# Memory stage of an encoder trunk: sums of squares by one-column matmuls, and another order of requests and reads

## The chip, the core and the metric

The kernel runs on one core of a Trainium2 chip. Its engines are TensorE (PE; its weight loads are shown as PEld), VectorE (DVE), ScalarE (ACT), GpSimd (POOL) and SyncE (SP), which issues most transfers. The metric is device time of one execution in microseconds.

## What is computed

Two layers of an encoder on 1024 tokens of width 1024. The change lies in the part that comes first: the projection of 256 memory tokens for both layers, and the first RMSNorm of the tokens.

```python
mem_n = rmsnorm(mem, norm_mem)
for i in range(DEPTH):
    h = rmsnorm(x, norm_mix[i])
    mkv = mem_n @ w_mem_kv[i]
    mk = mkv[..., :mw].reshape(B, N_MEM, N_MEM_HEADS, HEAD_DIM)
    mv = mkv[..., mw:].reshape(B, N_MEM, N_MEM_HEADS, HEAD_DIM)
    ...
    proj = h @ w_in_a[li]
    ...

def rmsnorm(x, g):
    x32 = x.astype(jnp.float32)
    y = x32 * lax.rsqrt(jnp.mean(x32 * x32, axis=-1, keepdims=True) + EPS)
    return (y * g.astype(jnp.float32)).astype(x.dtype)
```

After it come windowed attention with the first projection's results, memory attention, the output projection, a gated channel mixer, then the same with neighbourhood attention, and a last norm.

## The kernel before

All activations lie transposed: a tile has 128 features in its partitions and tokens along its free dimension. Tokens `x[k][f]` are 8 feature tiles by 2 halves of 512 tokens; memory tokens `memt` are 8 tiles of 256 tokens. A matrix product is made nearly exact in float32 by splitting each operand in a high part (a rounded copy, ScalarE, `hi`, L106) and a low part (the difference, VectorE, `lo`, L109), and by three products for each pair of tiles (`three`, `steps`, the matmul at L139). A dense unit has 8 feature tiles, so 24 products.

The memory stage works in the pool `mp`:

- The requests for memory tokens, the first weight unit `wm0`, the gains and the second unit go out first; unit 0's two halves are on ScalarE's queue, everything else on SyncE's.
- ScalarE multiplies each memory tile with its gain and rounds it (L293), VectorE makes the low part (L294). The product is made with tokens that are not yet normalized; the scale of the norm is applied to the result.
- `mem_norm` adds up squares: ScalarE squares a tile (L196), VectorE adds it to the sum so far (`merge`, L219), so that one tile is left. `mean` (L212) multiplies 128-column blocks of it, as weights, with a column of 1/1024, which leaves the mean square of each token in a partition. `scale` then adds epsilon (VectorE, L232), raises to the power -1/2 (GpSimd, L233), spreads the result over a diagonal (VectorE, L235) and broadcasts it by a product with ones (L242).
- A loop of eight units follows, four for each layer (two of keys, two of values). In round `i` it requests and splits unit `i + 2`, requests two or three token tiles, multiplies unit `i` (`dense`), and reads the result at once, with the scale (L337). Keys are split; values are transposed first (L344). Rounds 1 and 2 square the first token half, `norms[0]`; rounds 5 and 6 the second, `norms[1]`. From round 3 on, two tiles of the first half are normalized (L259) and split in each round.
- `first_dense` multiplies the first three units of the first projection with the first half (72 products 512 wide), while the second half is normalized; `first_units` in layer 0 then multiplies the same weights with the second half (72 more). The first score product of the attention (L559) comes after it.

A planner lays instructions out for each engine ahead of time; it keeps dependences, and takes what it expects to be ready in the order of the program. Each engine runs its list in that order and stops at what is not ready. A tag with `bufs` buffers gives a tile the buffer of an earlier one once that is done with: weights in split form (`whl`) have 3, unsplit ones (`raw`) 5, temporary tiles (`t2k`) 8. PSUM has 2 banks for `mm`, 2 for `S`, 3 for `T` and 1 for `O`; `mm_tile` gives results of units banks of the first three by turns, and the means of a norm hold a `T` bank until they are read.

The class `Norm` already has a number `summed`: tiles beyond that many are not added up but go to `mean` one by one. Its default is 8, all tiles.

```python
            self.acc.append(sq)
            if len(self.xs) > 2:
                self.merge()
```

Of the kernel before, what the change touches and what calls it, by code (L numbers as in the profile page):

```python
# [9 lines left out]
F32 = mybir.dt.float32  # L10
F32R = mybir.dt.float32r
AF = mybir.ActivationFunctionType
ALU = mybir.AluOpType
# [4 lines left out]
P = 128  # L18
D = 1024
S = 1024  # L20
NK = D // P
HS = 512
HD = 64
NH = 12
NKV = 4
NMH = 4
NM = 256
# [14 lines left out]
def trunk_kernel(ctx: ExitStack, tc: tile.TileContext, a: dict, out: bass.AP):  # L42
# [17 lines left out]
    nc = tc.nc  # L60
# [4 lines left out]
    wp = pool("wp", bufs=1)  # L65
# [4 lines left out]
    ps_t = pool("ps_t", bufs=3, space=PSUM)  # L70
    ps_o = pool("ps_o", bufs=1, space=PSUM)
# [10 lines left out]
    ident = cst.tile([P, P], F32, name="ident")  # L82
    gains = cst.tile([P, 6, NK], F32, name="gains")
    sink = cst.tile([P, NH], F32, name="sink")
    nsink = cst.tile([P, NH], F32, name="nsink")
    ones = cst.tile([P, P], F32, name="ones")
# [14 lines left out]
    def raw_tile(name):  # L101

        return phase[0].tile([P, D], F32, tag="raw", name=name, bufs=phase[2])

    def hi(dst, src):
        nc.scalar.copy(dst, src)  # L106

    def lo(dst, src, h, eng=None):
        (eng or nc.vector).tensor_tensor(dst, src, h.bitcast(F32), op=ALU.subtract)  # L109

    def load_w(src, tag="whl", bufs=3, eng=None, name="w", pool=wp, parts=1):
        raw = raw_tile(f"{name}_raw")
        nc.sync.dma_start(raw, src)
        w = pool.tile([P, 2, D], F32R, tag=tag, name=name, bufs=bufs)
        for i in range(parts):
            c = slice(i * D // parts, (i + 1) * D // parts)
            hi(w[:, 0, c], raw[:, c])
            pieces = 4 if eng is nc.gpsimd else 1
            for j in range(pieces):
                n = D // parts // pieces  # L120
                cj = slice(i * D // parts + j * n, i * D // parts + (j + 1) * n)
                lo(w[:, 1, cj], raw[:, cj], w[:, 0, cj], eng)
        return w
# [25 lines left out]
    def run_some(g, n):  # L149
        for _ in range(n):  # L150
            next(g, None)

    def first_dense(layer, norm):

        pre = []
        src = a["w_in_a"] if layer == 0 else a["w_in_b"]
        todo = (norm.add(x[k][1]) for k in range(len(norm.xs), NK))
        parts = norm.split(layer, hT[1])
        for n, u in enumerate(FIRST[layer]):
            w = load_w(src[u], eng=None if layer == 0 else nc.gpsimd, name="wf")  # L160
            wide[:] = True, 2 + n
            ps = mm_tile()
            for i, _ in enumerate(steps(ps, w, hT[0])):
                if next(todo, 0) is not None and len(norm.xs) == NK and (n or i > 3):
                    next(parts, None)
            pre.append((w, ps))
        run(parts)
        return pre
# [10 lines left out]
    def dense(w, h, n=HS):  # L179
        ps = mm_tile()  # L180
        run(steps(ps, w, h, n=n))
        return ps
# [85 lines left out]
    x = [[None, None] for _ in range(NK)]  # L268


    with tc.tile_pool(name="mp", bufs=1, reuse_waits="tile") as mp:
        phase[:] = mp, 8, 5
        memt = mp.tile([P, NK, NM], F32, name="memt")
        warm = mp.tile([P, P], F32, name="warm")
        nc.scalar.activation(warm, ones, AF.Square)
        wm0 = raw_tile("wm0")
        nc.sync.dma_start(memt[:, :2], a["mem"][:, :2])
        nc.scalar.dma_start(wm0[:, :HS], a["w_mem"][0, 0][:, :HS])
        nc.sync.dma_start(gains, a["gains"])
        nc.sync.dma_start(memt[:, 2:4], a["mem"][:, 2:4])  # L280
        nc.scalar.dma_start(wm0[:, HS:], a["w_mem"][0, 0][:, HS:])
        nc.sync.dma_start(memt[:, 4:], a["mem"][:, 4:])
        w0 = wp.tile([P, 2, D], F32R, tag="whl", name="wm", bufs=3)
        hi(w0[:, 0, :HS], wm0[:, :HS])
        lo(w0[:, 1, :HS], wm0[:, :HS], w0[:, 0, :HS])
        ws = [w0]


        mh = []
        mhl = mp.tile([P, NK, 2, NM], F32R, name="mhl")  # L290
        for k in range(NK):
            t, g = mhl[:, k], gains[:, 4, k : k + 1]
            nc.scalar.activation(t[:, 0], memt[:, k], AF.Copy, scale=g)  # L293
            nc.vector.scalar_tensor_tensor(  # L294
                t[:, 1], memt[:, k], g, t[:, 0].bitcast(F32), op0=ALU.mult, op1=ALU.subtract
            )
            mh.append(t)
            if k == 1:
                hi(w0[:, 0, HS:], wm0[:, HS:])
                lo(w0[:, 1, HS:], wm0[:, HS:], w0[:, 0, HS:])  # L300
        ws.append(load_w(a["w_mem"][0, 1], name="wm"))
        nc.sync.dma_start(ident, a["ident"])

        def load_x(f, k):
            x[k][f] = mp.tile([P, HS], F32, tag=f"x{k}{f}", name=f"x0_{k}{f}")
            nc.sync.dma_start(x[k][f], a["x"][k][:, f * HS : (f + 1) * HS])

        mem_norm = Norm(NM)
        for k in range(NK):
            mem_norm.add(memt[:, k])  # L310
        scale = mp.tile([P, NM], F32, name="mscale")
        nc.scalar.copy(scale, mem_norm.scale())

        hT = [[None] * NK, [None] * NK]
        norms = [Norm(), Norm()]
        kept = []
        for i in range(8):
            l, u = divmod(i, 4)
            if u == 0:
                kh = mp.tile([P, 2, NM], F32R, name=f"mkh{l}", tag="mkh", bufs=2)  # L320
                kl = mp.tile([P, 2, NM], F32R, name=f"mkl{l}", tag="mkl", bufs=2)
                vm = mp.tile([P, 2, NMH, 2, HD], F32R, name=f"mv{l}", tag="mv", bufs=2)
                kept.append((kh, kl, vm))
            if i + 2 < 8:
                ws.append(load_w(a["w_mem"][(i + 2) // 4, (i + 2) % 4], name="wm"))
            if i == 0:
                nc.sync.dma_start(sink, a["sink"].to_broadcast([P, NH]))
                nc.vector.tensor_scalar(nsink, sink, -1.0, None, op0=ALU.mult)
            if i < 3:
                for k in ((0, 1, 2), (3, 4, 5), (6, 7))[i]:  # L330
                    load_x(0, k)
            elif i < 7:
                for k in (2 * i - 6, 2 * i - 5):
                    load_x(1, k)
            ps = dense(ws[i], mh, NM)
            t = temp("mt", NM)
            nc.vector.tensor_tensor(t, ps[:, :NM], scale, op=ALU.mult)  # L337
            if u < 2:
                hi(kh[:, u], t)
                lo(kl[:, u], t, kh[:, u])  # L340
            else:
                tr = ps_t.tile([P, HS], F32, tag="T", name="mvT")
                for b in range(2):
                    nc.tensor.transpose(tr[:, b * P : (b + 1) * P], t[:, b * P : (b + 1) * P], ident)  # L344
                src = tr[:, :NM].rearrange("p (b i d) -> p b i d", b=2, i=2)
                m = 2 * (u - 2)
                for b in range(2):
                    hi(vm[:, b, m : m + 2, 0], src[:, b])
                    lo(vm[:, b, m : m + 2, 1], src[:, b], vm[:, b, m : m + 2, 0])
            if i in (1, 2):  # L350
                for k in range(4 * i - 4, 4 * i):
                    norms[0].add(x[k][0])
            if i == 2:
                parts = norms[0].split(0, hT[0])
            if i > 2:
                run_some(parts, 2)
            if i in (5, 6):
                for k in range(4 * i - 20, 4 * i - 16):
                    norms[1].add(x[k][1])
        pre = first_dense(0, norms[1])  # L360
        for l, (kh, kl, vm) in enumerate(kept):
            nc.sync.dma_start(memk_d[l, 0], kh.rearrange("p m k -> p (m k)").bitcast(F32))
            nc.sync.dma_start(memk_d[l, 1], kl.rearrange("p m k -> p (m k)").bitcast(F32))
            nc.sync.dma_start(memv_d[l], vm.rearrange("p b m i d -> p (b m i d)").bitcast(F32))

    for layer in range(2):
# [427 lines left out]
        with (  # L794
# [24 lines left out]
            norms = [Norm(), Norm()]  # L819
# [216 lines left out]
            for f in range(2):  # L1036
                for m in range(NK):
# [3 lines left out]
                    if f == 0 and m in po:  # L1041
                        w, ps = wo[m], po[m]
                        run(steps(ps, w, yT[f], [last_pair], start=False))
                    else:
                        ps = mm_tile("po")
                        w = wo[m] if f == 0 and m in wo else load_w(a["w_out"][layer, m], name="wo")
# [6 lines left out]
                    if f == 1 and m == 0:  # L1053
                        parts = norms[0].raw(2 + layer)
                    if f == 1:
                        k = next(parts)
# [114 lines left out]
            kept, left, right = {}, {}, {}  # L1171
# [181 lines left out]
            norms = [Norm(), Norm() if is_a else Norm(HS, 7)]  # L1353
            dorder = [(i, g) for i in (0, 1, 3, 2, 4, 5, 6) for g in range(len(groups))]
            parts = iter(())
# [124 lines left out]
```

## Time and profile before

| | us |
|---|---|
| three runs | 2146.28, 2148.43, 2148.71 |
| their median | 2148.43 |
| the profiled execution | 2144.64 |
| span of its instructions | 2142.7 |
| TensorE busy in that span | 2100.1 |
| first product of the memory stage | at 5.74 |
| first score product of layer 0 | at 83.90 |

The page of the profile gives busy times, the span in 40 slices of 54 us, the chain that ended last, and groups of instructions. The timeline gives runs of like instructions: start, time, engine, line, operation, result and operands, shape, count, and in brackets the idle time before them with what ended it. A view by windows gives busy time of the engines in a stretch, the granted TensorE clock and the load of the transfer engines. "L106" is line 106 of the kernel before.

### The profile page before, as it was taken

What the parts mean: (1) busy time and instruction counts of PE and PEld (TensorE: products, weight loads), DVE (VectorE), ACT (ScalarE), POOL (GpSimd) and SP (SyncE); (2) the same over time, 40 slices, a digit from 0 to 9 for tenths busy, and PEclk for the clock granted to TensorE, in tenths of its full rate; (3) what the DMA queues carried; (4) which work ended last, traced back from release to release, by engine and by line L of the source; (5) the groups of instructions that cost most, each with busy time, mean ns of one, the idle gap of its engine ahead of it and who ended that gap; (6) DMA issues with size and microseconds to landing.
All of it is one profiled execution on the core that took longest, in us unless ns stands there. A gap on an engine that the chain in (4) does not pass through costs nothing.

```text
span 2142.7 us, 28954 instructions
## 1 busy us (share of the span) xinstructions
PE 2100.1 (98%) x10270; PEld 1749.9 (82%) x10270; DVE 1514.4 (71%) x2466; ACT 1062.1 (50%) x2034; POOL 577.2 (27%) x617
## 2 busy tenths in 40 slices
PE   7999999999999999999999999999999999999997
PEld 6788888788888888888778888887888888888886
DVE  7677787788666666867766666667886666677675
ACT  6577785444433434344466566653443434344442
POOL 0344330334443430000233233203243444410000
PEclk9999999999999999999999999999999999999998
DMA  6321018323322336865232222265133323267562
GB/s 249 101 94 49 32 60 295 118 84 123 106 92 103 109 113 244 303 215 197 96 97 65 73 62 71 88 251 162 56 118 112 108 96 111 99 251 262 200 206 93
DMA packets 120080, 287.27 MB, mean 134 GB/s; under 512 B 12288, under 2 KB 18688, under 8 KB 119936
## 3 DMA queue, kind: packets, MB, share of 16 engines
q1 hardware_dynamic: 112896, 272.57, 37.5%
q10 hardware_dynamic: 7040, 12.85, 1.6%
q8 instruction: 81, 1.33, 0.3%
q14 instruction: 63, 0.52, 0.1%
HBM read 210.40 MB, written 68.94 MB: 130 GB/s over the span
## 4 chain that ended last, share of the span: by engine, by line
PE 77%; issue 13%; DVE 4%; ACT 3%; POOL 2%; DMA 1%; SPq 0%; DVEq 0%; ACTq 0%; POOLq 0%
PE X L885 16%; PE Y L885 16%; PE mm L139 14%; PE po L139 8%; PE X L1308 6%; PE Y L1308 4%; PE S L559 3%; PE O L622 3%; PE pT L602 3%; PE X L967 2%; PE Y L967 2%; ACT p L574 1%; DVE pl L109 1%; POOL wS L842 1%; DMA wm_raw<-in_w_mem 1%
## 5 line engine op out<-in xcount | busy, mean ns | idle before, releaser
L885 PE MATMUL Y<-hB,wgu 128*128 128x512 f32 x1056 | 256.1, 392 | 0.8 <-ACT c L905 0.8
L885 PE MATMUL X<-hB,wgu 128*128 128x512 f32 x1056 | 254.6, 390 | 0.0
L1308 PE MATMUL X<-hB,wd 128*128 128x512 f32 x1056 | 242.4, 390 | 1.1 <-DVE x L1276 1.1
L109 DVE TENSOR_TENSOR wgu<-wS,wgu 128x1024 fp32r<-128x1024 f32 (+1 forms) x124 | 152.9, 1233 | 124.9 <-ACT wgu L106 124.8
L1308 PEld LDWEIGHTS X<-hB,wd 128*128 128x128 f32 x1056 | 197.9, 188 | 43.2 <-issue 2.4
L885 PEld LDWEIGHTS Y<-hB,wgu 128*128 128x128 f32 x1056 | 196.6, 188 | 43.2 <-ACT c L905 1.6
L885 PEld LDWEIGHTS X<-hB,wgu 128*128 128x128 f32 x1056 | 196.1, 188 | 40.0
L587 POOL TENSOR_SCALAR p<-p,stat 128x384 f32<-128x384 f32 (+1 forms) x256 | 140.9, 569 | 314.5 <-DVE stat L584 205.2
L139 PE MATMUL mm<-hT,wqk 128*128 128x512 f32 x672 | 199.9, 405 | 0.1
L106 ACT CAST wgu<-wS 128x1024 fp32r<-128x1024 f32 (+1 forms) x124 | 114.3, 923 | 148.6 <-POOL wS L842 124.5
L139 PE MATMUL po<-yT,wo 128*128 128x512 f32 x768 | 184.7, 394 | 0.0
L1308 PE MATMUL Y<-hB,wd 128*128 128x512 f32 x792 | 180.4, 389 | 0.0
L1308 PEld LDWEIGHTS Y<-hB,wd 128*128 128x128 f32 x792 | 148.6, 188 | 31.2 <-DVE x L1276 0.3
L233 POOL TENSOR_TENSOR nr<-nv,neg_half 128x4 f32<-128x4 f32 (+1 forms) x11 | 11.7, 1063 | 597.6 <-DVE nv L232 597.5
L139 PEld LDWEIGHTS po<-yT,wo 128*128 128x128 f32 x768 | 142.4, 188 | 29.6 <-issue 1.0
L885 PE MATMUL X<-hT,wgu 128*128 128x512 f32 x624 | 150.1, 391 | 0.0
L106 ACT CAST hB<-b_raw 128x512 fp32r<-128x512 f32 x154 | 89.5, 618 | 110.8 <-DMA b_raw<-b_d 97.4
L842 POOL TENSOR_TENSOR wS<-wgu_raw 128x512 f32<-128x512 f32 x44 | 61.0, 1386 | 294.5 <-DVE wgu L109 294.5
L574 ACT ACTIVATE p<-p,stat 128x256 f32<-128x256 f32 (+1 forms) x192 | 112.3, 586 | 52.6 <-DVE stat L570 49.9
L885 PEld LDWEIGHTS X<-hT,wgu 128*128 128x128 f32 x624 | 116.9, 188 | 26.1
L109 DVE TENSOR_TENSOR pl<-pT,ph 128x384 fp32r<-128x384 f32 (+1 forms) x256 | 118.7, 494 | 21.0 <-ACT ph L106 17.9
L109 DVE TENSOR_TENSOR hB<-b_raw,hB 128x512 fp32r<-128x512 f32 x154 | 100.0, 688 | 42.3 <-ACT hB L106 42.0
(179 smaller groups left out, 4229.6 us busy)
## 6 DMA issues: line engine op xcount, KB each, us to landing
wgu_raw<-in_w_gu SPq DMA_DIRECT2D x92, 512.0 KB
wd_raw<-in_w_dn SPq DMA_DIRECT2D x70, 512.0 KB
b_raw<-b_d SPq DMA_DIRECT2D x70, 512.0 KB
b_d<-c SPq DMA_DIRECT2D x88, 256.0 KB
b_d<-t SPq DMA_DIRECT2D x66, 256.0 KB
wo_raw<-in_w_out SPq DMA_DIRECT2D x32, 512.0 KB
x<-in_x SPq DMA_DIRECT2D x32, 256.0 KB
xr_d<-x ACTq DMA_DIRECT2D x32, 256.0 KB
```

What stands on the lines that cost most here:

```text
L106: nc.scalar.copy(dst, src)
L109: (eng or nc.vector).tensor_tensor(dst, src, h.bitcast(F32), op=ALU.subtract)
L139: nc.tensor.matmul(ps[:, :n], l, r, start=start and i == 0 and j == 0, stop=stop and i == len(order) - 1 and j == 2,)
L559: nc.tensor.matmul(s_[:, :n], Q[self.h][:, qb * P : (qb + 1) * P], k, start=j == 0, stop=j == 1)
L574: nc.scalar.activation(p[:, :n], p[:, :n], AF.Exp, bias=m1, scale=-1.0, accum_out=s1)
L587: nc.gpsimd.tensor_scalar(p[:, :n], p[:, :n], ri[:, i : i + 1], 1.0, op0=ALU.mult, op1=ALU.mult)
L602: nc.tensor.transpose(tr[:, j * P : (j + 1) * P], p[:, j * P : (j + 1) * P], ident)
L622: nc.tensor.matmul(o[:, c0 : c0 + w * P], self.value(j), t[:, s0 : s0 + w].rearrange("p j q -> p (j q)"), start=j == js[0] and t is self.p ...
L842: sub = lambda o, p_, q_: nc.gpsimd.tensor_tensor(o, p_, q_, op=ALU.subtract)
L885: nc.tensor.matmul(ps, l, r, start=n in (0, 1, 3, 6) and k == 0 and i == 0, stop=k == 3 and i == 2, skip_group_check=True,)
L967: nc.tensor.matmul(bank[:, at : at + h2], l, r, start=start and k == 0 and i == 0, stop=stop and k == 1 and i == 2, skip_group_check=True,)
L1308: nc.tensor.matmul(bank, l, r, start=i in (0, 1, 3, 6) and p == 0 and n == 0, stop=p == HF - 1 and n == 2, skip_group_check=True,)
```

## The change

- Five products of `ones` with `ones` stand at the head of TensorE's list.
- Token requests are made for two feature tiles at once (512 KB) and stand earlier: the four of the first half between those of weight units 1, 2 and 3, the four of the second half with units 4 to 7. Weight units are requested four rounds ahead (before: two), and still split two rounds ahead.
- The three norms of the stage are made with `summed` 0: every squared tile goes to `mean` itself, and no `merge` is left in them.
- Squaring of the first token half stands ahead of the products of rounds 1 and 2, before behind them. The scale of the memory norm stands behind the product of round 2, before ahead of the loop.
- Results are read in a function of their own, `finish_wm`: unit 0 in round 2, unit `i - 2` in each later round, units 6 and 7 after the loop.
- The request for the sink logits stands behind those of unit 3 and of the first token half.

```diff
@@ -273,21 +273,50 @@
         memt = mp.tile([P, NK, NM], F32, name="memt")
         warm = mp.tile([P, P], F32, name="warm")
         nc.scalar.activation(warm, ones, AF.Square)
-        wm0 = raw_tile("wm0")
+        for _ in range(5):
+            nc.tensor.matmul(ps_o.tile([P, HS], F32, tag="O", name="warm")[:, :P], ones, ones, start=True, stop=True)
+
+        def load_wm(i):
+            ws[i] = raw_tile("wm")
+            nc.sync.dma_start(ws[i], a["w_mem"][i // 4, i % 4])
+
+        def split_wm(i, cs=slice(0, D)):
+            if i not in whl:
+                whl[i] = wp.tile([P, 2, D], F32R, tag="whl", name="wm", bufs=3)
+            w = whl[i]
+            hi(w[:, 0, cs], ws[i][:, cs])
+            lo(w[:, 1, cs], ws[i][:, cs], w[:, 0, cs])
+
+        def load_x(f, k):
+            t = mp.tile([P, 2, HS], F32, tag=f"x{k}{f}", name=f"x0_{k}{f}")
+            nc.sync.dma_start(
+                t, a["x"][k : k + 2].rearrange("m p t -> p m t")[:, :, f * HS : (f + 1) * HS]
+            )
+            x[k][f], x[k + 1][f] = t[:, 0], t[:, 1]
+
+        ws, whl = {}, {}
+        ws[0] = raw_tile("wm0")
         nc.sync.dma_start(memt[:, :2], a["mem"][:, :2])
-        nc.scalar.dma_start(wm0[:, :HS], a["w_mem"][0, 0][:, :HS])
+        nc.scalar.dma_start(ws[0][:, :HS], a["w_mem"][0, 0][:, :HS])
         nc.sync.dma_start(gains, a["gains"])
         nc.sync.dma_start(memt[:, 2:4], a["mem"][:, 2:4])
-        nc.scalar.dma_start(wm0[:, HS:], a["w_mem"][0, 0][:, HS:])
+        nc.scalar.dma_start(ws[0][:, HS:], a["w_mem"][0, 0][:, HS:])
         nc.sync.dma_start(memt[:, 4:], a["mem"][:, 4:])
-        w0 = wp.tile([P, 2, D], F32R, tag="whl", name="wm", bufs=3)
-        hi(w0[:, 0, :HS], wm0[:, :HS])
-        lo(w0[:, 1, :HS], wm0[:, :HS], w0[:, 0, :HS])
-        ws = [w0]
+        load_wm(1)
+        load_x(0, 0)
+        load_x(0, 2)
+        load_wm(2)
+        nc.sync.dma_start(ident, a["ident"])
+        load_x(0, 4)
+        load_x(0, 6)
+        load_wm(3)
+        nc.sync.dma_start(sink, a["sink"].to_broadcast([P, NH]))
+        split_wm(0, cs=slice(0, HS))


         mh = []
         mhl = mp.tile([P, NK, 2, NM], F32R, name="mhl")
+        mem_norm = Norm(NM, 0)
         for k in range(NK):
             t, g = mhl[:, k], gains[:, 4, k : k + 1]
             nc.scalar.activation(t[:, 0], memt[:, k], AF.Copy, scale=g)
@@ -296,67 +325,64 @@
             )
             mh.append(t)
             if k == 1:
-                hi(w0[:, 0, HS:], wm0[:, HS:])
-                lo(w0[:, 1, HS:], wm0[:, HS:], w0[:, 0, HS:])
-        ws.append(load_w(a["w_mem"][0, 1], name="wm"))
-        nc.sync.dma_start(ident, a["ident"])
-
-        def load_x(f, k):
-            x[k][f] = mp.tile([P, HS], F32, tag=f"x{k}{f}", name=f"x0_{k}{f}")
-            nc.sync.dma_start(x[k][f], a["x"][k][:, f * HS : (f + 1) * HS])
-
-        mem_norm = Norm(NM)
+                split_wm(0, cs=slice(HS, D))
+        split_wm(1)
         for k in range(NK):
             mem_norm.add(memt[:, k])
+        nc.vector.tensor_scalar(nsink, sink, -1.0, None, op0=ALU.mult)
+
+        hT = [[None] * NK, [None] * NK]
+        norms = [Norm(HS, 0), Norm(HS, 0)]
         scale = mp.tile([P, NM], F32, name="mscale")
-        nc.scalar.copy(scale, mem_norm.scale())
-
-        hT = [[None] * NK, [None] * NK]
-        norms = [Norm(), Norm()]
-        kept = []
-        for i in range(8):
-            l, u = divmod(i, 4)
-            if u == 0:
-                kh = mp.tile([P, 2, NM], F32R, name=f"mkh{l}", tag="mkh", bufs=2)
-                kl = mp.tile([P, 2, NM], F32R, name=f"mkl{l}", tag="mkl", bufs=2)
-                vm = mp.tile([P, 2, NMH, 2, HD], F32R, name=f"mv{l}", tag="mv", bufs=2)
-                kept.append((kh, kl, vm))
-            if i + 2 < 8:
-                ws.append(load_w(a["w_mem"][(i + 2) // 4, (i + 2) % 4], name="wm"))
-            if i == 0:
-                nc.sync.dma_start(sink, a["sink"].to_broadcast([P, NH]))
-                nc.vector.tensor_scalar(nsink, sink, -1.0, None, op0=ALU.mult)
-            if i < 3:
-                for k in ((0, 1, 2), (3, 4, 5), (6, 7))[i]:
-                    load_x(0, k)
-            elif i < 7:
-                for k in (2 * i - 6, 2 * i - 5):
-                    load_x(1, k)
-            ps = dense(ws[i], mh, NM)
+        kept, sums = [], {}
+
+        def finish_wm(i):
+
+            (kh, kl, vm), u, ps = kept[i // 4], i % 4, sums.pop(i)
             t = temp("mt", NM)
             nc.vector.tensor_tensor(t, ps[:, :NM], scale, op=ALU.mult)
             if u < 2:
                 hi(kh[:, u], t)
                 lo(kl[:, u], t, kh[:, u])
-            else:
-                tr = ps_t.tile([P, HS], F32, tag="T", name="mvT")
-                for b in range(2):
-                    nc.tensor.transpose(tr[:, b * P : (b + 1) * P], t[:, b * P : (b + 1) * P], ident)
-                src = tr[:, :NM].rearrange("p (b i d) -> p b i d", b=2, i=2)
-                m = 2 * (u - 2)
-                for b in range(2):
-                    hi(vm[:, b, m : m + 2, 0], src[:, b])
-                    lo(vm[:, b, m : m + 2, 1], src[:, b], vm[:, b, m : m + 2, 0])
+                return
+            tr = ps_t.tile([P, HS], F32, tag="T", name="mvT")
+            for b in range(2):
+                nc.tensor.transpose(tr[:, b * P : (b + 1) * P], t[:, b * P : (b + 1) * P], ident)
+            src = tr[:, :NM].rearrange("p (b i d) -> p b i d", b=2, i=2)
+            m = 2 * (u - 2)
+            for b in range(2):
+                hi(vm[:, b, m : m + 2, 0], src[:, b])
+                lo(vm[:, b, m : m + 2, 1], src[:, b], vm[:, b, m : m + 2, 0])
+
+        parts = iter(())
+        for i in range(8):
+            if i % 4 == 0:
+                l = i // 4
+                kh = mp.tile([P, 2, NM], F32R, name=f"mkh{l}", tag="mkh", bufs=2)
+                kl = mp.tile([P, 2, NM], F32R, name=f"mkl{l}", tag="mkl", bufs=2)
+                vm = mp.tile([P, 2, NMH, 2, HD], F32R, name=f"mv{l}", tag="mv", bufs=2)
+                kept.append((kh, kl, vm))
+            if i + 4 < 8:
+                load_wm(i + 4)
+                load_x(1, 2 * i)
+            if i + 2 < 8:
+                split_wm(i + 2)
             if i in (1, 2):
                 for k in range(4 * i - 4, 4 * i):
                     norms[0].add(x[k][0])
+            sums[i] = dense(whl[i], mh, NM)
             if i == 2:
+                nc.scalar.copy(scale, mem_norm.scale())
+                finish_wm(0)
                 parts = norms[0].split(0, hT[0])
             if i > 2:
+                finish_wm(i - 2)
                 run_some(parts, 2)
             if i in (5, 6):
                 for k in range(4 * i - 20, 4 * i - 16):
                     norms[1].add(x[k][1])
+        finish_wm(6)
+        finish_wm(7)
         pre = first_dense(0, norms[1])
         for l, (kh, kl, vm) in enumerate(kept):
             nc.sync.dma_start(memk_d[l, 0], kh.rearrange("p m k -> p (m k)").bitcast(F32))
```

## The prediction

> **What bounds the kernel now.** I read the page first, then busy time by stretches, the timeline of TensorE, and last the groups of the stage that the change touches.
>
> ```profile
> span 2142.7 us, 28954 instructions
> PE 2100.1 (98%) x10270; PEld 1749.9 (82%) x10270; DVE 1514.4 (71%) x2466; ACT 1062.1 (50%) x2034; POOL 577.2 (27%) x617
> PE   7999999999999999999999999999999999999997
> PE 77%; issue 13%; DVE 4%; ACT 3%; POOL 2%; DMA 1%; SPq 0%; DVEq 0%; ACTq 0%; POOLq 0%
> ```
>
> TensorE is busy for 98% of the span and holds 77% of the chain. A microsecond that it loses or wins in the memory stage therefore moves the end by a microsecond, unless it later waits for something that has its own date; nothing with such a date shows. Only the first slice of 54 us is below 9, and that is the stage in question. These stretches cut it at the events named below:
>
> ```profile
> core 0: us, PE busy (x) PEld busy (x) DVE busy (x) ACT busy (x) POOL busy (x), PEclk, DMA share, GB/s
> 22.70:24.60 1.90, 0.00 (x0) 0.00 (x0) 1.66 (x5) 1.90 (x5) 0.00 (x0) 1.00 1.03 400
> 24.60:25.80 1.20, 0.00 (x0) 0.00 (x0) 1.20 (x4) 1.20 (x3) 0.00 (x0) 0.50 1.04 388
> 25.80:34.80 9.00, 8.78 (x36) 8.09 (x37) 5.08 (x10) 1.44 (x3) 1.01 (x1) 0.50 0.94 360
> 34.80:60.00 25.20, 21.88 (x127) 17.26 (x126) 22.58 (x39) 14.21 (x26) 1.85 (x1) 1.00 0.21 68
> 60.00:83.90 23.90, 23.90 (x106) 19.71 (x105) 15.74 (x24) 10.99 (x18) 4.69 (x6) 1.00 0.54 166
> ```
>
> TensorE stands still from 22.7 to 25.8; in the middle of that the granted clock falls to 0.50 and stays there for 9.0 us of work, half of which (4.5 us) is lost. From 34.8 to 60 VectorE is busy 22.6 of 25.2 us and TensorE has holes. After 60 it is full. The rows of TensorE behind it:
>
> ```profile
> 5.74 6.07 PE L139 MATMUL mm<-mhl,wm 128*128 128x256 f32 x26 [5.74 <-ACT mhl L293]
> 25.81 2.38 PE L139 MATMUL mm<-mhl,wm 128*128 128x256 f32 x5 [3.19 <-ACT wm L106]
> 46.46 2.56 PE L139 MATMUL mm<-hT,wf 128*128 128x512 f32 x10 [1.44 <-DVE wf L109]
> 51.46 1.53 PE L139 MATMUL mm<-hT,wf 128*128 128x512 f32 x5 [0.32 <-DVE hT L109]
> 54.40 0.44 PE L344 MATMUL mvT<-ident,mt 128*128 128x128 f32 x2 [1.41 <-DVE mt L337]
> 59.69 24.38 PE L139 MATMUL mm<-hT,wf 128*128 128x512 f32 x105
> 83.90 0.28 PE L559 MATMUL S<-mKH,QS 128*128 128x256 f32 x1
> ```
>
> The stage ends where the first score product starts, at 83.90; from the first product at 5.74 that is 78.2 us. How much of it is work comes from the distance from one weight load to the next, since recorded durations overlap:
>
> ```profile
> 14.47 0.53 PEld L212 LDWEIGHTS st<-inv_d,sq 128*128 128x128 f32 x4
> 14.92 0.42 PEld L139 LDWEIGHTS mm<-mhl,wm 128*128 128x128 f32 x3
> 28.61 1.78 PEld L212 LDWEIGHTS st<-inv_d,sq 128*128 128x128 f32 x8
> 30.27 4.17 PEld L139 LDWEIGHTS mm<-mhl,wm 128*128 128x128 f32 x19
> 35.55 5.76 PEld L139 LDWEIGHTS mm<-mhl,wm 128*128 128x128 f32 x48 [0.24 <-issue]
> 55.00 1.01 PEld L212 LDWEIGHTS st<-inv_d,sq 128*128 128x128 f32 x8
> 55.93 2.84 PEld L139 LDWEIGHTS mm<-hT,wf 128*128 128x128 f32 x13
> 16.91 0.30 PEld L242 LDWEIGHTS bc<-diag,ones 128*128 128x128 f32 x2 [0.55 <-DVE diag L235]
> 59.12 0.30 PEld L242 LDWEIGHTS bc<-diag,ones 128*128 128x128 f32 x2 [0.36 <-DVE diag L235]
> 59.66 0.19 PEld L139 LDWEIGHTS mm<-hT,wf 128*128 128x128 f32 x1 [0.24 <-issue]
> ```
>
> A 256-wide memory product costs 5.76/48 = 0.12 us, a 512-wide one 24.38/105 = 0.232. A one-column product of a sum of squares (tile st) costs (14.92-14.47)/4 = 0.113 at the first place and (55.93-55.00)/8 = 0.116 at the last; I take 0.115. Although it moves one column, it pays for loading 128 columns of weights. At half clock it is (30.27-28.61)/8 = 0.21. A broadcast pair takes about 59.66-59.12 = 0.54, the short one for 256 columns about 0.35, a transpose about a load, 0.12. Work of the stage: 192 x 0.12 = 23.0, 144 x 0.232 = 33.4, 20 x 0.115 = 2.3, 8 x 0.12 = 1.0, broadcasts 1.4; together 61.1 us. **Lost: 78.2 - 61.1 = 17.1 us.** That is all that the change can win here. It consists of the first unit (6.24 us up to 11.98 less 26 x 0.12 = 3.1), the stop before 25.81 (3.2), the half clock (4.5), three waits for VectorE after 35 (1.44 + 0.32 + 1.41 = 3.2), waits before broadcasts, and small ones.
>
> **The change part by part.** The groups of the stage:
>
> ```profile
> L219 DVE TENSOR_TENSOR sq<-sq 128x512 f32<-128x512 f32 x14 | 9.1, 687 | 0.3 <-ACT sq L196 0.3
> L219 DVE TENSOR_TENSOR sq<-sq 128x256 f32<-128x256 f32 x7 | 2.5, 420 | 0.0
> L212 PE MATMUL st<-inv_d,sq 128*128 128x1 f32 x20 | 3.3, 281 | 0.0
> ```
>
> *Sums of squares.* All 21 additions of squares leave VectorE, 9.1 + 2.5 = 11.6 us. In their place each of 24 squared tiles goes through TensorE: two blocks for each of 8 memory tiles, four for each of 16 token tiles, so 80 products in place of 10. The trace shows 20 instructions for those 10, so two each: 160 in place of 20. The 140 added cost 140 x 0.115 = **16.1 us of TensorE**. Between 0.113 and 0.116 that is 15.8 to 16.2; at half clock up to 29; below, nothing, if each load hid under a neighbour. I take the row, because it was paid beside 256-wide and beside 512-wide neighbours alike. [...]
>
> *Tokens sooner.* By the tiles' shapes SyncE's queue holds, up to the last token tile of the first half, 1 MB of memory tokens, weight units 0 to 4 (2.5 MB) and 2 MB of tokens. Afterwards it holds units 0 to 2 only, so 1 MB less; at the 400 GB/s of the stretch at 22.7 the tokens land about 2.6 us sooner. Units 2 and 3 move behind 1 MB and 1.25 MB more, 2.6 and 3.3 us later, and the 16 token requests become 8.
>
> ```profile
> 13.04 1.03 ACT L106 CAST wm<-wm_raw 128x1024 fp32r<-128x1024 f32 x1
> 16.11 1.05 ACT L106 CAST wm<-wm_raw 128x1024 fp32r<-128x1024 f32 x1 [2.03 <-DMA wm_raw<-in_w_mem]
> 13.86 0.17 DVE L328 TENSOR_SCALAR nsink<-sink 128x12 f32<-128x12 f32 x1
> 10.58 2.56 ACT L196 ACTIVATE sq<-memt 128x256 f32<-128x256 f32 x8
> ```
>
> The casts at 13.04 and 16.11 are of units 2 and 3. Unit 2 would then be cast by 15.6 at the latest and its low part ready near 18; TensorE reaches it after unit 1 and 32 instructions of the memory sums, at about 11.98 + 2.9 + 2.7 = 17.6. Unit 3 is cast by 19.5, and TensorE is there about 8 us later, after the first four tokens' sums (32 x 0.115 = 3.7), unit 2 (2.9) and the next four (3.7). So the later weights cost about nothing; without that cover they cost up to 3.3 us.
>
> *Products read later.* Nothing is added: the same eight reads, casts and transposes. The reads no longer stand ahead of the splits in VectorE's queue; eight sums occupy banks longer, and two or three banks of each tag suffice, as each is read before its tag comes round. What it frees is the wait on the scale, which is not on the path of the rows above.
>
> *Five products on a constant.* At two instructions each and 0.21 at half clock they last 2.1 us, while TensorE waits until 5.74 for the first memory tile. They cost nothing. They can raise the clock before the first unit; but that is paced by ScalarE and VectorE splitting memory tiles until about 10.3, and unit 1 needs its low part at 11.98. What they win is at most the 1 us in which sums of memory tiles (squared from 10.58 on) can now fill the hole before 11.98.
>
> *Sink.* Its sign change on VectorE (13.86) stands ahead of the splits of units 2 and on, while the request moves behind 2.5 MB more in SyncE's queue, 6.6 us. If VectorE waits there until about 20, the low part of unit 2 is ready near 21.8 instead of 17.6, 4 us late; the first four tokens' sums (3.7) need nothing from VectorE and can cover that if they come first in TensorE's order. I take nothing, and leave the 4 us to rival 2.
>
> **The sum.** TensorE's work becomes 61.1 + 16.1 = 77.2. To this come the losses that stay: the first unit 3.1 - 1.0 = 2.1; three broadcasts, each behind a chain through VectorE and GpSimd, 3 x 0.35 = 1.0 (rows 0.55 and 0.36, less the load's lead); half of the 3.2 us of waits for VectorE, 1.6, since it sheds 11.6 us but 16 splits of tokens (two operations of 0.7 each) stay between the sums and the products; and 1.0 for waits that the new order brings (bounds: none, and the 3.2 of the stop at 22.7). Together 5.7. The stop and the half clock go, because the added products fill them. 77.2 + 5.7 = 82.9 against 78.2: **4.7 us slower.** The profiled execution took 2144.64 us, 1.9 more than its span, and would take 2149.3. It lies under all three runs shown (2146.28 to 2148.71), so I add to their median of 2148.43: **2153.1 us**.
>
> **The rivals.** (1) *The losses nearly vanish.* VectorE keeps ahead everywhere and only the first unit and a wait or two remain, 3.5 us: 77.2 + 3.5 - 78.2 = +2.5, 2150.9 us. For it speaks VectorE's 11.6 us of relief, against it that TensorE's order is fixed beforehand and met every late operand so far with a stop. (2) *A new stop.* VectorE waits for the sink, or ScalarE stands at a weight unit with token squares behind it; TensorE idles 2 to 4 us and the clock drops again. In the rows, 1.9 us without work sufficed for that. The losses are then 5.7 + 2 + half of a stretch of 6 to 9 us at half clock: +10, 2158.4. [...] (3) *The other side: the one-column products hide.* Place: sums beside 512-wide products, where loads of 0.115 come only every 0.232, so one more load fits under each. Price: up to 16.1. It decides from 9.0 us hidden on (4.7 + 4.3), that is 78 of the 140; with two thirds hidden, -6.0, 2142.4 us. For it: weight loads are busy only 19.71 of 23.90 us after 60. Against it: sums come four or eight in a row, and no 512-wide product can precede the first tokens' sums, which leaves 64. (4) *It does not do what it says:* tokens come no sooner, as the queues were full (share 1.04). The path then still carries the 16.1, so this gives the forecast or (2).
>
> **How the numbers follow.** About 0.2%, 4.3 us, is what a measurement of this kernel can tell from no change. Forecast 0.42 (its own range 4.3 to 8 us, 2152.7 to 2156.5), rival 1 0.37, rival 2 0.13, rival 3 0.08; (4) is held in the first and third. Slower: 0.42 + 0.13 = 0.55; same 0.37; faster 0.08. The range leaves out rival 3 and the far end of rival 2 and goes from no change, which the lower bound of the added products less the rows' waits allows, to rival 2: 2148.0 to 2158.5.
>
> **What would show it.** Right: 160 instructions of st, 0.11 to 0.12 apart; no addition of squares before 60; no half clock between 20 and 40; first score product near 88.6. Wrong: that product before 84 (rival 3, or work counted twice), or after 92 (rival 2, with its stop in TensorE's rows). The forecast fails if st loads are under 0.06 apart, or if later stages shift by themselves.

## The result, and the profile after

| | before | after |
|---|---|---|
| median of four runs, us | 2148.57 | 2160.69 |
| profiled execution | 2144.64 | 2158.95 |
| its span | 2142.7 | 2157.2 |
| first memory product | 5.74 | 5.87 |
| first score product | 83.90 | 100.57 |

The changed kernel is slower by 12.1 us: its time is 1.006 of that before, 95% interval 1.0048 to 1.0072. The forecast was 4.7 us slower, with 10 at the end of its range. The page of the changed kernel:

```profile
span 2157.2 us, 29216 instructions
PE 2126.2 (99%) x10420; PEld 1778.1 (82%) x10420; DVE 1504.2 (70%) x2445; ACT 1060.0 (49%) x2034; POOL 577.8 (27%) x617
PE   9999999999999999999999999999999999999997
PEclk7999999999999999999999999999999999999998
```

TensorE's first slice has gone from 7 to 9: the holes are filled, and still the stage is longer. The other line to read is the clock, 7 in that slice; on the page of the kernel before, it is 9:

```profile
PEclk9999999999999999999999999999999999999998
```

Cut where the granted clock changes, the changed kernel's stage is this (us of the stretch, busy time of each engine with its instructions, granted clock, load of the transfer engines, GB/s):

```profile
core 0: us, PE busy (x) PEld busy (x) DVE busy (x) ACT busy (x) POOL busy (x), PEclk, DMA share, GB/s
9.50:16.30 6.80, 6.80 (x60) 6.70 (x59) 2.28 (x5) 6.80 (x16) 0.07 (x1) 1.00 1.05 394
16.30:40.20 23.90, 23.90 (x113) 23.72 (x112) 4.58 (x9) 5.07 (x10) 3.57 (x2) 0.50 0.52 192
40.20:60.70 20.50, 20.50 (x159) 19.42 (x159) 19.30 (x32) 14.62 (x26) 0.00 (x0) 1.00 0.40 126
60.70:64.10 3.40, 3.40 (x11) 2.72 (x11) 1.84 (x4) 1.51 (x4) 0.00 (x0) 0.50 0.18 67
64.10:67.50 3.40, 3.40 (x30) 3.27 (x28) 0.76 (x2) 0.00 (x0) 0.00 (x0) 1.00 0.23 87
67.50:74.30 6.80, 6.80 (x24) 5.73 (x24) 1.74 (x6) 0.99 (x4) 1.01 (x1) 0.50 0.01 5
```

TensorE is busy in every microsecond, and yet 23.9 + 3.4 + 6.8 = 34.1 us run at half clock, against 10.2 before. From the first product to the first score product the stage takes 94.7 us. If everything at half clock took exactly twice as long, half of the 34.1, **17.1 us, would be the loss**; 94.7 - 17.1 = 77.6 would remain, the 77.2 us of work that the prediction had counted and 0.4 of all other waits. This is the upper end: e3 below makes the same number of sums at full clock, and its stage takes 84.99 - 5.90 = 79.1 us, which puts the loss at 15.6. Which instructions stand in those stretches is seen in the same view for the line of the sums (L212) alone:

```profile
core 0: us, PE busy (x) PEld busy (x), PEclk, DMA share, GB/s
9.50:16.30 6.80, 3.98 (x32) 4.10 (x33) 1.00 1.05 394
16.30:40.20 23.90, 13.61 (x64) 14.39 (x64) 0.50 0.52 192
64.10:67.50 3.40, 2.81 (x26) 3.01 (x25) 1.00 0.23 87
```

The clock falls right after stretches that are full of one-column products, 32 of 60 instructions and 26 of 30, and it stays low while they go on, 64 of 113 instructions from 16.3 to 40.2. It was not so before: there it fell in a stop, after 1.90 us without any product. At half clock one of them takes nearly twice the 0.113 us of full clock, as the weight loads of the changed kernel show, (25.18 - 21.77)/16 = 0.213 us; a 256-wide product beside them takes (31.80 - 30.09)/8 = 0.214, against 0.12 at full clock:

```profile
21.77 3.53 PEld L212 LDWEIGHTS st<-inv_d,sq 128*128 128x128 f32 x16
25.18 0.76 PEld L139 LDWEIGHTS mm<-mhl,wm 128*128 128x128 f32 x3
30.09 1.83 PEld L139 LDWEIGHTS mm<-mhl,wm 128*128 128x128 f32 x8
31.80 1.82 PEld L212 LDWEIGHTS st<-inv_d,sq 128*128 128x128 f32 x8
```

Some 2.2 us come back behind the stage: its end is 16.7 us later, the span 14.5 us longer. Before, TensorE had a hole at 89.5 and a stretch at half clock behind it; these are its rows, then those of the changed kernel at about the same distance from its first score product:

```profile
89.46:92.88 3.42, 1.58 (x10) 0.87 (x9) 0.85 (x2) 2.24 (x7) 3.42 (x7) 1.00 0.00 0
92.88:96.30 3.42, 3.42 (x12) 2.94 (x13) 1.52 (x6) 1.25 (x4) 3.09 (x5) 0.50 0.00 0
```

```profile
106.00:110.00 4.00, 3.97 (x26) 3.14 (x25) 3.01 (x11) 3.23 (x12) 2.11 (x5) 1.00 0.05 19
110.00:114.00 4.00, 3.90 (x24) 2.90 (x24) 3.23 (x8) 3.61 (x13) 1.58 (x4) 1.00 0.01 4
```

### The profile page after: what moved, and what is told of

It reads as the page before. It is cut to its first block, busy times and chain, and to the rows that moved or that the text cites. A ratio compares the mean times of both kernels' runs of the same rounds, so it can differ in the third digit from the quotient of the medians.

```text
span 2157.2 us, 29216 instructions
## 1 busy us (share of the span) xinstructions
PE 2126.2 (99%) x10420; PEld 1778.1 (82%) x10420; DVE 1504.2 (70%) x2445; ACT 1060.0 (49%) x2034; POOL 577.8 (27%) x617
## 4 chain that ended last, share of the span: by engine, by line
PE 77%; issue 14%; DVE 4%; ACT 3%; POOL 1%; DMA 1%; DVEq 0%; ACTq 0%; POOLq 0%
PE X L911 16%; PE Y L911 15%; PE mm L139 15%; PE po L139 6%; PE X L1334 5%; PE Y L1334 4%; PE S L585 3%; PE O L648 3%; PE pT L628 3%; PE X L993 2%; PE Y L993 2%; PE st L212 1%; ACT p L600 1%; DVE pl L109 1%; POOL wS L868 1%
## 5 line engine op out<-in xcount | busy, mean ns | idle before, releaser
L106 ACT CAST hB<-b_raw 128x512 fp32r<-128x512 f32 x154 | 89.5, 618 | 109.6 <-DMA b_raw<-b_d 91.3
L109 DVE TENSOR_TENSOR pl<-pT,ph 128x384 fp32r<-128x384 f32 (+1 forms) x256 | 119.1, 494 | 20.5 <-ACT ph L106 17.1
L911 PE MATMUL Y<-hT,wgu 128*128 128x512 f32 x528 | 129.9, 391 | 0.0
```

The costliest lines, as they stand in the source:

```text
L911: nc.tensor.matmul(ps, l, r, start=n in (0, 1, 3, 6) and k == 0 and i == 0, stop=k == 3 and i == 2, skip_group_check=True,)
```

## The experiments

Theory A: one-column products occupy TensorE but move almost nothing through it, and the clock is granted by what moves. Theory B: the clock falls by the new order of requests and reads, whatever the products are. All kernels but e2 start from the changed kernel. "Half clock" is that of the profiled execution, in us, between the first rise of the clock (at 9.5 to 12.6 us) and 80 us; the last column is read from the same execution.

| | median | before, beside it | ratio, 95% interval | half clock | first score product |
|---|---|---|---|---|---|
| e1 sums undone | 2141.97 | 2145.97 | 0.9982 (0.9973 to 0.9991) | 10.2 | 83.10 |
| e2 sums alone, in the kernel before | 2160.11 | 2145.97 | 1.0068 (1.0051 to 1.0085) | 23.9 | 98.02 |
| e3 sums of 64 columns | 2147.83 | 2145.97 | 1.0008 (0.9999 to 1.0018) | 0 | 84.99 |
| e4 no products on a constant | 2164.49 | 2145.97 | 1.0081 (1.0065 to 1.0097) | 34.1 | 101.10 |
| e5 sums of 16 columns | 2154.58 | 2146.45 | 1.0043 (1.0027 to 1.0059) | 27.3 | 99.34 |
| e6 second half wide | 2143.81 | 2146.45 | 0.9982 (0.9974 to 0.9991) | 0 | 81.73 |
| e7 memory and second half wide | 2144.17 | 2146.45 | 0.9986 (0.9978 to 0.9995) | 0 | 81.95 |
| e8 e1 with reads at once | 2145.67 | 2146.45 | 0.9998 (0.9990 to 1.0007) | 6.8 | 83.89 |
| e9 as e3, this stage alone | 2145.01 | 2147.10 | 0.9992 (0.9983 to 1.0001) | 0 | 84.63 |
| e10 as e6, this stage alone | 2141.44 | 2147.10 | 0.9974 (0.9963 to 0.9985) | 0 | 81.67 |
| e11 e1, no constant | 2142.50 | 2147.10 | 0.9978 (0.9969 to 0.9987) | 10.2 | 82.99 |
| e12 sums of 32 columns | 2146.10 | 2146.66 | 1.0002 (0.9988 to 1.0016) | 0 | 85.93 |

**e1, the sums undone.**

```diff
-        mem_norm = Norm(NM, 0)
+        mem_norm = Norm(NM)
-        norms = [Norm(HS, 0), Norm(HS, 0)]
+        norms = [Norm(), Norm()]
```

> The changed kernel with its three norms back on additions by VectorE (20 one-column instructions instead of 160); all else as changed. Theory A (one-column products occupy TensorE but move almost no columns, so the granted clock falls): at most 4 us at half clock between 12 and 60; first score product near 74 (61 us of work, some 7 lost); 2137 to 2144 us. Theory B (the clock falls because of the new order of requests and reads, whatever the products are): still 15 us or more at half clock before 60; first score product after 84; 2150 to 2156 us.

The time fell to 4.0 us under the kernel before: the sums cost more than the whole loss, and the rest of the change is a gain. The clock stays up until 47.9, so B is out for the long stretch. But A's 74 for the first score product was missed by 9 us, and its 4 us of half clock at most became 10.2: VectorE, with its additions back, lets TensorE wait, and then the clock falls too (windows of e1, and the row of TensorE in the middle of it):

```profile
40.00:47.90 7.90, 6.18 (x23) 3.78 (x21) 7.90 (x15) 5.76 (x11) 0.00 (x0) 1.00 0.24 85
47.90:58.10 10.20, 9.22 (x24) 6.25 (x25) 6.31 (x14) 1.40 (x5) 1.85 (x1) 0.50 0.48 162
```

```profile
48.56 1.09 PE L350 MATMUL mvT<-ident,mt 128*128 128x128 f32 x4 [1.23 <-DVE mt L343]
```

VectorE works all of 7.90 us, TensorE 6.18.

**e2, the sums alone**, in the kernel before.

```diff
-        mem_norm = Norm(NM)
+        mem_norm = Norm(NM, 0)
-        norms = [Norm(), Norm()]
+        norms = [Norm(HS, 0), Norm(HS, 0)]
```

> The kernel before with nothing but its three norms changed to one-column products for every tile. Theory A: 15 us or more at half clock before 70, where the kernel before has 10.2; first score product 12 to 20 us later than 83.9; 2159 to 2168 us. Theory B: the products fill the stop at 22.7 and the clock stays up; first score product 0 to 6 us later; 2148 to 2155 us.

That is the whole loss, 14.1 us, without one line of the new order. The windows of e2 show the clock down, up and down again, and TensorE is never idle in these rows:

```profile
14.80:21.60 6.80, 6.80 (x33) 6.62 (x32) 1.96 (x4) 0.65 (x2) 0.71 (x1) 0.50 1.04 407
21.60:28.50 6.90, 6.90 (x62) 6.90 (x61) 4.24 (x7) 4.91 (x9) 0.00 (x0) 0.99 1.02 386
28.50:35.30 6.80, 6.80 (x34) 6.80 (x34) 0.29 (x1) 2.93 (x6) 0.00 (x0) 0.50 0.30 96
```

**e3, sums of 64 columns.** The same number of instructions and of weight loads; the column of 1/1024 becomes 64 equal columns (`WC = 64`).

```diff
-    inv_d = cst.tile([P, 1], F32, name="inv_d")
+    inv_d = cst.tile([P, WC], F32, name="inv_d")
 ...
-                    self.st[:, b : b + 1], sq[:, b * P : (b + 1) * P], inv_d,
+                    self.st[:, b * WC : (b + 1) * WC], sq[:, b * P : (b + 1) * P], inv_d,
 ...
+            st = st.rearrange("p (b c) -> p b c", c=WC)[:, :nb, 0]
```

> The changed kernel with the column of 1/1024 made 64 columns wide, so that each of the 160 instructions moves 64 columns instead of one, with the same weight loads; the other columns are copies that nobody reads (norms of later stages get them too). Theory A: the clock stays at full speed nearly throughout before 75, an instruction costs 0.11 to 0.15 us, first score product at 83 to 89; 2143 to 2150 us, though more columns are moved. Theory B: the clock falls as in the changed kernel, and the time is the same or longer: 2160 to 2166 us.

This run decides. Doing 64 times as much with the sums, the kernel stands at 1.0008 of the kernel before where the changed one stands at 1.006, some 11 us faster, and its clock stays up (windows of e3, then its sums and a row of weight loads in the same stage):

```profile
10.10:40.00 29.90, 29.90 (x252) 29.37 (x251) 16.84 (x28) 17.70 (x33) 3.63 (x2) 1.00 0.82 297
40.00:60.00 20.00, 19.96 (x135) 17.83 (x134) 14.83 (x29) 11.24 (x24) 1.85 (x1) 1.00 0.26 94
60.00:85.00 25.00, 25.00 (x112) 20.66 (x112) 13.91 (x22) 10.93 (x18) 8.18 (x10) 1.00 0.56 164
```

```profile
L213 PE MATMUL st<-inv_d,sq x160: 217/275/323, 11.2 to 53.5; 128*128 128x64 f32 x160
```

```profile
20.87 3.66 PEld L213 LDWEIGHTS st<-inv_d,sq 128*128 128x128 f32 x32
24.44 2.94 PEld L140 LDWEIGHTS mm<-mhl,wm 128*128 128x128 f32 x24
```

From 10.1 to 40 TensorE gets through 252 instructions; the changed kernel needs its 23.9 us at half clock for 113. One sum of 64 columns takes (24.44 - 20.87)/32 = 0.112 us by its weight loads, no more than the 0.113 of a single column: with the same loads, the columns do not change the price. All 160 are there, so what the changed kernel loses against e3 is the clock, not their work. The planner laid the list out anew, so the order differs too, but it is no gentler: here 32 sums stand in one row, in the changed kernel at most 16.

**e5 and e12, how wide.** `WC = 16` and `WC = 32` in the edit of e3.

> As e3, but 16 columns instead of 64. [...] Theory D (anything wider than one column counts as a full product): clock as in e3, 2145 to 2150 us.

> As e3 and e5, with 32 columns. [...] The stretch of e3 kept the clock, that of e5 lost it. [...] No preference; the run narrows it.

16 columns lose the clock from 16.0 to 43.3 (e5's windows), and keep it in the second half, where the sums stand beside 512-wide products and the changed kernel lost it twice:

```profile
16.00:43.30 27.30, 27.30 (x128) 27.12 (x128) 5.55 (x11) 6.04 (x11) 3.63 (x2) 0.50 0.48 176
43.30:75.00 31.70, 31.14 (x220) 28.09 (x220) 23.88 (x45) 16.58 (x33) 1.01 (x1) 1.00 0.31 108
```

e5's seven times spread from 2149.65 to 2163.37, e12's ten lie between 2144.79 and 2146.74 but for one of 2159.22. The mean granted clock over an execution is 0.988 to 0.994 in e5's seven, 0.996 or 0.997 in e3's ten, and 0.997 or 0.998 in e12's but for 0.991 in the one of 2159.22. So with 16 columns every execution was longer at the lower clock than any with 64, and with 32 one of ten was; theory D is out.

A count of columns comes close to telling where the clock falls. In all fourteen traces the clock keeps a value for whole steps of 3.41 us (10.2 us is three in the kernel before, 23.9 seven in the changed one). The table counts, from the clock's first rise to 100 us, the moving columns of the products that start in each step:

| clock in the step | and after it | steps | moving columns in each |
|---|---|---|---|
| half | full | 18 | 2560 or more |
| half | half | 30 | 2400 or fewer |
| full | full | 310 | 2560 or more, but for one (2304, e12) |
| full | half | 18 | 2560 or fewer, but for two (3344 in the changed kernel, 3089 in e4, both near 13 us) |

Steps of 256-wide products alone have some 7000. By this count the stop before the change is like the sums: its step, from 21.2, has 2304 columns, while one from 51.9, in which TensorE stood still for 1.4 us, has 2819 and kept the clock. The count was made after the runs and none was built to test it; what exactly is counted stays open.

**e4 and e11, the products on a constant.** The loop of five is taken out, of the changed kernel and of e1.

> The changed kernel without the five products on a constant. Theory A: full clock comes one or two steps of 3.4 us later than 9.5, first score product 0 to 2 us later; 2160 to 2163 us. Theory C (the five products raise the clock early and it must fall again after a fixed time): the time at half clock before 60 is shorter by 5 us or more; 2153 to 2158 us.

> As e1 without the five products on a constant. If they matter: full clock a step of 3.4 us later, 1 to 3 us slower than e1. If the first unit is paced by the splitting of memory tiles alone: within 1 us of e1.

e11 and e1 stand at 0.9978 and 0.9982, so there the five products have no effect that shows. e4's 2164.49 lies above the 2160 to 2163 expected, and its interval overlaps the changed kernel's: a loss of some microseconds without the five is possible, and not shown. In e4 the clock rises at 9.9 instead of 9.5, stays down for the same 34.1 us, and theory C is out.

**e8, reads at once**, on top of e1: the scale ahead of the loop, `finish_wm(i)` behind product `i`.

```diff
+        nc.scalar.copy(scale, mem_norm.scale())
 ...
             sums[i] = dense(whl[i], mh, NM)
+            finish_wm(i)
 ...
-                finish_wm(i - 2)
 ...
```

> As e1, but each memory product read at once and the scale ahead of the loop, as in the kernel before; what is left of the change is the order of requests, squares ahead of products, and the five products. If the later reads bring the gain of e1: a stop of TensorE and half clock between 15 and 40 again, 2 to 6 us slower than e1. If the order of requests does: within 1.5 us of e1.

3 us of e1's 4 are gone, with the half clock again at 17.5 (window of e8) and once more at 55.0:

```profile
17.50:20.90 3.40, 3.40 (x17) 3.40 (x18) 2.64 (x7) 3.40 (x8) 0.00 (x0) 0.50 1.04 396
```

But its first score product comes only 0.8 us after e1's; the greater part is lost behind it, with half clock from 92.6 to 96.0 as in the kernel before. Why the later reads spare that was not tried. The two intervals touch, so this is likely and not more.

**e6, e7, e9, e10, a better kernel.** The squares of the second token half alone go to TensorE, 64 wide, where e1 waits for VectorE; e7 adds the memory tokens. e9 and e10 are e3 and e6 with the wide columns for this stage only; in e3, e6 and e7 the later norms have them too. In e10 the edit of the stage is this:

```diff
-        mem_norm = Norm(NM, 0)
+        mem_norm = Norm(NM)
 ...
-        norms = [Norm(HS, 0), Norm(HS, 0)]
+        norms = [Norm(), Norm(HS, 0, 64)]
```

> As e1 (additions by VectorE), but the squares of the second token half by TensorE with 64 columns as in e3: 56 more products, seven fewer additions. Theory A with the sum over engines: TensorE has 61.1 + 56 x 0.113 = 67.4 us of work, VectorE loses 4.8 us where e1 has TensorE waiting for it and the clock falls at 47.9; no half clock before 75, first score product 78 to 81 against 83.1; 5 to 9 us under the kernel before. Rival (the splits of tokens on VectorE set that stretch, not the additions): within 1.5 us of e1, with the half clock still there.

> As e6, and the squares of the memory tokens by TensorE too: 28 more products, 3.2 us, in a stretch where TensorE of e1 stands still for about 3 us (15.0 to 21). Theory A: within 2 us of e6, no half clock. If the products come ahead of units that are on the path: 2 to 4 us slower than e6.

> As e3 (64 columns for all three norms of the memory stage), but the later norms keep one column. e3's time from the first gate product (at 406) to the end was 1738.8 us, against 1734.7 before; if the wide columns of later norms make that, this ends 3 to 5 us earlier than e3: 2 to 4 us under the kernel before, first score product again near 85, no half clock before 100. If the later part differs by itself from build to build: as e3, 0 to 3 us over the kernel before.

> As e6 (additions for memory and the first token half, TensorE with 64 columns for the second), but the later norms keep one column. If the wide columns of later norms cost e6 its gain (from the first gate product on 1740.4 us against 1734.7): first score product near 81.7 and 6 to 9 us under the kernel before, faster than e1. If not: as e6, 2 to 4 us under it.

The half clock of e1 at 47.9 goes, and the first score product comes at 81.7, just after the 78 to 81 expected. But e6 came out only 2.6 us under the kernel before, not 5 to 9, and no earlier than e1: from the first gate product on it took 1740.4 us, e1 1734.7. With the wide columns only here, e10 took 1736.2 and came out 5.7 us under the kernel before, a little short of the 6 to 9 expected. TensorE's clock holds from its first rise to 2123.8. Its windows:

```profile
10.60:40.00 29.40, 25.58 (x196) 23.74 (x195) 26.54 (x47) 20.17 (x40) 2.65 (x2) 1.00 0.81 297
40.00:60.00 20.00, 19.75 (x120) 16.91 (x120) 15.71 (x31) 10.42 (x22) 1.01 (x1) 1.00 0.36 124
```

For e9 and e3 the evidence is mixed: by their medians e9 lies 2.1 us under the kernel before and e3 1.9 over it, but in the profiled executions they take 1738.0 and 1738.8 us from the first gate product on. The later part also differs by stretches at half clock that the edits do not aim at (3.4 us from 1048 in e6 and from 412 in e9, none in e10). So e10 beats the kernels before and after, but its lead over e1 is not shown: the two intervals overlap. e7's 28 memory products neither helped nor hurt.

## Why the prediction was wrong

The direction was right, the size was not: 12.1 us measured, 4.7 forecast, 10 at the end of the range.

- *The price and number of the sums* were right: 160 instructions, 0.112 us apart, and at full clock a stage of 77.6 (reckoned) to 79.1 us (e3) against 77.2 of work. That it was paid in full, beside other products, was right too; rival 3 (loads hidden) would have been further off: the traces show 0.112 to 0.116 us for each at full clock, in the kernel before and in e3.
- *The waits* were taken too high. 5.7 us were kept for the first unit, the broadcasts, VectorE and the new order; 0.4 to 1.9 were left, as TensorE always had a sum or a product at hand. The later weight units and the sink cost nothing; the sink's sign change was laid behind the sums, at 36.4. The squares of the first half did come sooner, the last ending at 18.2 and before at 24.8, so rival (4) is out.
- **The step that failed** is in the sum: "The stop and the half clock go, because the added products fill them." The stop went. The half clock grew from 10.2 to 34.1 us, at a price of 15.6 to 17.1 us where the prediction had none, and its own sign of being right, no half clock between 20 and 40, failed. It took a busy TensorE for a full clock. e2 shows it with the sums alone, e3 with their number and loads unchanged and the clock back: -5.3 us for waits and +17.1 for the clock, or by e3 -3.8 and +15.6, are the 11.8 us by which the stage (16.5 us longer) missed 4.7.
- Rival 2 had the end of the range and the wrong mechanism: it wanted an idle TensorE for the lower clock, and there is none in the rows (23.90 of 23.90 us busy at 0.50). Its price was too small as well: 3 to 4.5 us for the clock, where the half clock cost some four times that.
- That the profiled execution lies under the medians did not matter; some 2 us of the stage's loss came back behind it, which nothing in the prediction had.

## What to carry to other kernels

Before small products are moved to TensorE, ask two prices: their weight loads (here 0.113 us for one column), and what the clock makes of a stretch that they fill; the second was paid here by the 256-wide products beside them too, 0.214 us instead of 0.12. A row of busy TensorE is no evidence of full speed: 23.90 of 23.90 us were busy at a granted clock of 0.50; read the clock beside it. Where such products are needed, widening the moving operand to 64 columns cost no more for each product here (0.112 us in e3) and kept the clock (1.00 from 10.1 to 85.0).

## What the hardware showed

In the changed kernel the granted clock fell to 0.50 with TensorE busy for 6.80 of 6.80 us, and stayed there for 23.9 us of unbroken work. A product of 64 float32 columns with a weight load of its own cost 0.112 us (e3), no more than one of a single column with 0.113 (the kernel before). With 16 columns the mean granted clock was 0.988 to 0.994 in all seven executions, below the 0.996 or 0.997 of e3's ten with 64; with 32 it was so in one of ten, 0.991; the edits changed only the width, and with it the order that the planner made. At 16 the same program spreads over 14 us. In the fourteen traces, the steps of 3.41 us at half clock after which it rose held 2560 moving columns or more (18 steps), and those after which it stayed down 2400 or fewer (30 steps).
